# Storing the last sixteen tiles in other pieces: a different spread of short stores over the DMA engines, and another order of the early adds

## The chip, the cores and the metric

The kernel runs on one core of one Trainium2 chip. The metric is the device time of one execution in microseconds (us), as the median of the runs shown. The core has sixteen DMA engines; their queue is fed here by one engine, SyncE (SP), in the order of its program.

## The reference

The kernel computes a batched matrix product with a bias and a residual, all in fp32:

```
x: (16, 512, 1024)   weight: (1024, 768)   bias: (768,)   residual: (16, 512, 768)
out = np.matmul(x, weight) + bias + residual
```

Flattened, that is 8192 rows. It reads 32 MB of x, 24 MB of residual and 3 MB of weights, and it writes 24 MB.

## The kernel before, in words

The 8192 rows are cut into 64 tiles of 128 rows (partitions), and the tiles into four groups S of J = 16. Tile t = 16·S + j. A partition's sixteen rows of a group lie next to each other in memory, so one transfer can load or store any run of tiles j0 to j1 of a group with one contiguous piece per partition. A piece is 4 KB per tile for x and 3 KB per tile for the residual and the output.

Three fixed buffers hold the data. `X` has 16 slots of x. `R` has 32 rows of 768 fp32 values: row t mod 32 holds the residual of tile t, becomes its output in place, and is stored from there. The weights are first loaded into eight rows of `R` from row `W_ROW` on (`w_st`, line 86), and are then cast to bf16 into `w_sb`.

Each tile passes through the same steps. ACT casts x to bf16 (`cast`, L149). PE transposes it as four 128x128 fp32 blocks (`transp`, L157) and VectorE (DVE) copies the result out of PSUM (L158). Sixteen matmuls accumulate into one of three PSUM tiles (`mm`, L164). GpSimd (POOL) adds the bias to the residual row ahead of time (L189), and DVE adds the PSUM result to that row (`finish`, L199).

The first fourteen tiles (`EARLY_END`) are done in another way, because their residuals come late. DVE adds the bias to the PSUM result and puts it in a temporary row of `R` (`tmp(t)`, row 16 + t, L195). POOL later adds that row to the residual row (L185). `ADDS` lists tiles 0 to 15; in it stands the order in which POOL takes those adds. `pool_adds(upto)` is called as the program is written out. It walks that list over the tiles up to `upto`, emits the adds whose inputs have been scheduled, and stops at the first that has not. So the list and the point of the call together decide POOL's order.

All transfers are issued by SP in the order of `ORDER`. The entries are `('x', S, j0, j1)`, `('r', ...)`, `('w', ...)` and `('b', ...)` for loads, and `('s', S, j0, j1)` for a store. A fifth number in a store cuts it into two transfers at that partition. `('c', 3, 15, i)` stores the two column pieces of tile 63, 512 and 256 columns wide (`LAST`). `pump` (L91) emits an entry as soon as what it needs has been emitted. A load into a slot of `R` waits for the add or the store that last used the slot. The load of residual tiles 16 to 21, `('r', 1, 0, 6)`, overwrites the temporary rows of tiles 0 to 5, and so it waits for the adds of these six tiles. The load of tiles 22 to 31 waits for the adds of tiles 6 to 13.

SP works in program order. A transfer that waits holds up every transfer behind it. Transfers that have been issued lie in sixteen queues, one for each DMA engine, and each engine works through its own queue in order.

Of the kernel before, what the change touches and what calls it, by code (L numbers as in the profile page):

```python
# [19 lines left out]
WARM = 12  # L20
EARLY_END = 14
TMP_ROW = 16
W_ROW = 14
ADDS = [10, 14, 3, 2, 4, 15, 11, 1, 5, 13, 7, 6, 12, 9, 0, 8]
HEAD_ORDER = [('cast', 0, 'v'), ('cast', 1, 's'), ('tr', 0), ('tr', 1), ('wc', 0, 0, 's'), ('wc', 0, 1, 'g'),
 ('warm', 3), ('mm', 0, 0), ('mm', 1, 0), ('cast', 2, 'sv'), ('cast', 3, 'sv'), ('warm', 3),
 ('tr', 2), ('tr', 3), ('wc', 1, 0, 's'), ('wc', 1, 1, 'v'), ('mm', 2, 0), ('mm', 0, 1),
# [5 lines left out]
 ('r', 0, 6, 16), ('x', 0, 14, 16), ('x', 1, 0, 6), ('r', 1, 0, 6), ('x', 1, 6, 16),  # L33
 ('r', 1, 6, 16), ('s', 0, 0, 16), ('x', 2, 0, 6), ('r', 2, 0, 6), ('x', 2, 6, 16),
 ('r', 2, 6, 16), ('s', 1, 0, 16), ('x', 3, 0, 6), ('r', 3, 0, 7), ('x', 3, 6, 16),
 ('r', 3, 7, 16), ('s', 2, 0, 16), ('s', 3, 0, 10), ('s', 3, 10, 12, 108), ('s', 3, 12, 14),
 ('s', 3, 14, 15), ('c', 3, 15, 0), ('c', 3, 15, 1)]
LAST = [(0, 512), (512, 256)]


# [1 line left out]
def kernel(  # L42
# [42 lines left out]
    K_ = tc.keep_in_program_order  # L85
    w_st = R[:, W_ROW:W_ROW + 2 * n_q, :]

# [3 lines left out]
    def pump():  # L91
        while queue:
# [7 lines left out]
            elif kind == "r":  # L100
                need = [("store", t - RR) for t in range(J * S + j0, J * S + j1) if t >= RR]
                rows = [t % RR for t in range(J * S + j0, J * S + j1)]
                if S < RR // J and any(W_ROW <= r < W_ROW + 2 * n_q for r in rows):
                    need.append(("wcast", n_q - 1))
# [70 lines left out]

    adds = list(ADDS) + list(range(max(ADDS) + 1, n_t))

# [119 lines left out]
```

## Time and profile before

| | before |
|---|---|
| median of 8 runs | 210.76 us (210.54 to 210.88) |
| the profiled execution | 210.54 us, of which its span is 208.8 us |
| granted TensorE clock, mean | 0.996 |
| PE busy | 202.0 us, 97% of the span |
| POOL, DVE, ACT busy | 115.9, 104.7, 66.1 us |
| the data queue's packets | 87.05 MB, 97.9% of 16 engines' span |
| stores (L130) | ten transfers |

Busy times are the sum of an engine's instructions in one profiled execution. The share of a DMA queue is the time of its packets over the span of all sixteen engines. SPq is SP's queue of DMA issues: a line with it tells when a transfer was ordered, not when its data moved. Span and execution differ by 1.74 us, which lies around the profiled instructions.

### The profile page before, as it was taken

Reading aid. Unit: us, or ns where it says so; the run is one execution under the profiler, and the core shown is the slowest. Engines: PE = TensorE matmul, PEld = TensorE weight load, DVE = VectorE, ACT = ScalarE, POOL = GpSimd, SP = SyncE. Lnnn points to the kernel's source line nnn. Section 1 sums busy time; section 2 is a strip of 40 time slices with the busy share of each in tenths; the row PEclk is TensorE's granted clock in tenths of the full one; section 3 lists DMA queues with packets and bytes.
Section 4 is the critical chain, followed back from the end, with each engine's and each line's share of the span. In section 5 each row is a group of like instructions: output and inputs, shape, how many; then the busy total and the mean of one; then the engine's idle time right before and its main releaser. Section 6 shows DMA issues by size and latency. Waiting matters only on the chain.

```text
span 208.8 us, 3113 instructions
## 1 busy us (share of the span) xinstructions
PE 202.0 (97%) x1298; PEld 130.1 (62%) x1298; DVE 104.7 (50%) x140; ACT 66.1 (32%) x69; POOL 115.9 (56%) x72
## 2 busy tenths in 40 slices
PE   7999999999999999999999999999999999999990
PEld 2455666666666666666666666666666666666660
DVE  0458555445545543654455454645545544654551
ACT  2444513402640372420380094320091046440000
POOL 2100029859999804999029701999207950699400
PEclk9999999999999999999999999999999999999998
DMA  6999999999989899999999999999999999998985
GB/s 234 427 425 433 430 431 453 400 452 420 478 379 488 387 430 413 444 419 427 425 446 457 405 430 471 405 427 405 426 487 411 416 426 468 448 444 371 421 356 203
DMA packets 4780, 87.24 MB, mean 418 GB/s; under 512 B 538, under 2 KB 666, under 8 KB 1694
## 3 DMA queue, kind: packets, MB, share of 16 engines
q1 hardware_dynamic: 4766, 87.05, 97.9%
q8 instruction: 10, 0.16, 0.3%
q14 instruction: 4, 0.03, 0.0%
HBM read 61.88 MB, written 25.17 MB: 417 GB/s over the span
## 4 chain that ended last, share of the span: by engine, by line
PE 92%; DMA 4%; ACT 1%; DVE 1%; SPq 0%; issue 0%
PE psum_o L164 78%; PE pt L157 13%; DMA x_tile<-in_x_dram 4%; PE psum_o L258 1%; ACT xb L146 1%; DVE xt L158 0%; DVE ro L262 0%; SPq L119 0%; SPq L122 0%
## 5 line engine op out<-in xcount | busy, mean ns | idle before, releaser
L164 PE MATMUL psum_o<-w_sb,xt 128*128 128x512 bf16 x1008 | 174.0, 326 | 0.5 <-DVE xt L158 0.3
L164 PEld LDWEIGHTS <-xt 128*128 128x128 bf16 x1008 | 98.5, 98 | 59.2 <-DVE xt L158 0.7
L189 POOL TENSOR_TENSOR ro<-ro,bias_sb 128x768 f32<-128x768 f32 x50 | 88.9, 1823 | 48.4 <-DMA ro<-in_residual_dram 38.0
L149 ACT CAST xb<-x_tile 128x1024 bf16<-128x1024 f32 x60 | 59.7, 1043 | 113.8 <-DMA x_tile<-in_x_dram 87.2
L158 DVE COPY xt<-pt 128x1024 bf16<-128x1024 bf16 x64 | 44.0, 691 | 83.2 <-PE pt L157 83.2
L199 DVE TENSOR_TENSOR ro<-psum_o,ro 128x768 f32<-128x768 f32 x49 | 46.5, 948 | 5.9 <-POOL ro L189 4.8
L185 POOL TENSOR_TENSOR ro<-ro 128x768 f32<-128x768 f32 x14 | 25.0, 1820 | 25.2 <-DMA ro<-in_residual_dram 25.2
L157 PE MATMUL pt<-ident,xb 128*128 128x128 f32 x256 | 38.4, 274 | 0.4 <-ACT xb L146 0.2
L157 PEld LDWEIGHTS pt<-ident,xb 128*128 128x128 f32 x256 | 29.7, 141 | 9.0 <-ACT xb L146 1.1
L195 DVE TENSOR_TENSOR ro<-psum_o,bias_sb 128x768 f32<-128x768 f32 x14 | 13.2, 947 | 0.0
L208 PE MATMUL psum_o<-warm 128*128 128x512 bf16 x12 | 5.0, 602 | 1.2 <-DVE warm_a L204 1.2
L229 ACT CAST w_sb<-ro 128x768 bf16<-128x768 f32 x4 | 3.3, 832 | 3.7 <-DMA ro<-in_weight_dram 3.7
L208 PEld LDWEIGHTS <-warm 128*128 128x128 bf16 x12 | 1.6, 144 | 3.9 <-issue 2.8
L229 POOL CAST w_sb<-ro 128x768 bf16<-128x768 f32 x1 | 0.8, 823 | 5.4 <-DMA ro<-in_weight_dram 5.4
L149 DVE CAST xb<-x_tile 128x1024 bf16<-128x1024 f32 x1 | 0.7, 694 | 4.3 <-DMA x_tile<-in_x_dram 4.3
L146 ACT CAST xb<-x_tile 128x512 bf16<-128x512 f32 x3 | 1.8, 616 | 3.4 <-PE psum_o L164 1.7
L258 PE MATMUL psum_o<-w_sb,xt 128*128 128x512 bf16 (+1 forms) x16 | 2.8, 326 | 0.0
L229 DVE CAST w_sb<-ro 128x768 bf16<-128x768 f32 x3 | 1.7, 557 | 2.0 <-DMA ro<-in_weight_dram 2.0
L147 DVE CAST xb<-x_tile 128x512 bf16<-128x512 f32 x3 | 1.2, 425 | 2.6 <-DMA x_tile<-in_x_dram 2.6
L258 PEld LDWEIGHTS <-xt 128*128 128x128 bf16 x16 | 1.6, 98 | 1.1
L223 PE MATMUL psum_o<-warm 128*128 128x512 bf16 x6 | 1.6, 379 | 0.0
L262 DVE TENSOR_TENSOR ro<-psum_o,ro 128x512 f32<-128x512 f32 (+1 forms) x2 | 1.1, 559 | 0.9 <-PE psum_o L258 0.8
(14 smaller groups left out, 5.1 us busy)
## 6 DMA issues: line engine op xcount, KB each, us to landing
out_dram<-ro SPq DMA_DIRECT2D x3, 6144.0 KB, 34.6
x_tile<-in_x_dram SPq DMA_DIRECT2D x3, 5120.0 KB, 24.1
ro<-in_residual_dram SPq DMA_DIRECT2D x3, 3840.0 KB, 25.6
x_tile<-in_x_dram SPq DMA_DIRECT2D x3, 3072.0 KB, 40.7
ro<-in_residual_dram SPq DMA_DIRECT2D x3, 2304.0 KB, 17.6
x_tile<-in_x_dram SPq DMA_DIRECT2D x4, 1024.0 KB, 8.2
x_tile<-in_x_dram SPq DMA_DIRECT2D x2, 2048.0 KB, 21.2
out_dram<-ro SPq DMA_DIRECT2D x1, 3840.0 KB
```

The lines of the kernel that those rows point to most:

```text
L146: K_(nc.scalar.copy(out=dst[:, 0:K // 2], in_=src[:, 0:K // 2]))
L149: K_((nc.scalar.copy if how == "s" else nc.vector.tensor_copy)(out=dst, in_=src))
L157: K_(nc.tensor.transpose(out=pt[:, q, :], in_=words[:, ts(q, P)], identity=ident))
L158: K_(nc.vector.tensor_copy(out=XT[t % XT_N].rearrange("p q m e -> p (q m e)"), in_=pt.rearrange("p q m -> p (q m)").bitcast(BF16),))
L164: K_(nc.tensor.matmul(PO[t % HEAD][:, n0:n0 + nl], lhsT=XT[t % XT_N][:, q, :, e], rhs=w_sb[:, q, e, n0:n0 + nl], start=(q == 0 and e == 0) ...
L185: K_(nc.gpsimd.tensor_add(out=r, in0=r, in1=tmp(t)))
L189: K_(nc.gpsimd.tensor_add(out=r, in0=r, in1=bias_sb))
L195: K_(nc.vector.tensor_add(out=tmp(t), in0=p, in1=bias_sb))
L199: K_(nc.vector.tensor_add(out=row(t), in0=p, in1=row(t)))
L208: K_(nc.tensor.matmul(PO[0][:, 0:512], lhsT=warm[:, 0:P], rhs=warm, start=True, stop=True))
L229: K_(copy(out=w_sb[:, q, e, :], in_=w_st[:, 2 * q + e, :]))
L258: K_(nc.tensor.matmul(p, lhsT=XT[t % XT_N][:, q, :, e], rhs=w_sb[:, q, e, n0:n0 + nl], start=(q == 0 and e == 0), stop=(q == n_q - 1 and e ...
```

## The change

Three things are edited.

The weights are staged in rows 24 to 31 of `R` rather than in rows 14 to 21.

The list `ADDS` is another permutation of 0 to 15. Written out, POOL's first sixteen adds stood in the order 0, 1, 3, 2, 4, 5, 7, 6, 10, 11, 14, 15, 13, 12, 9, 8. Now they stand in the order 0, 1, 4, 5, 3, 9, 7, 2, 8, 14, 12, 10, 15, 13, 11, 6. From tile 16 on nothing changes.

The stores of the last group (tiles 48 to 63) are cut in other places. Before, tiles 48 to 57 went in one transfer of 128 rows, tiles 58 and 59 as 108 and 20 rows, 60 and 61 in one, 62 in one, and 63 in two column pieces. Now tile 48 goes by itself as 100 and 28 rows, 49 to 52 in one transfer, 53 to 59 in one, 60 and 61 in one, 62 as 126 and 2 rows, and 63 in two column pieces as before. There are twelve stores where there were ten. The instructions of PE, DVE and ACT keep their order.

```diff
-W_ROW = 14
-ADDS = [10, 14, 3, 2, 4, 15, 11, 1, 5, 13, 7, 6, 12, 9, 0, 8]
+W_ROW = 24
+ADDS = [4, 1, 5, 14, 9, 3, 7, 15, 12, 2, 8, 10, 13, 11, 6, 0]
...
- ('r', 3, 7, 16), ('s', 2, 0, 16), ('s', 3, 0, 10), ('s', 3, 10, 12, 108), ('s', 3, 12, 14),
- ('s', 3, 14, 15), ('c', 3, 15, 0), ('c', 3, 15, 1)]
+ ('r', 3, 7, 16), ('s', 2, 0, 16), ('s', 3, 0, 1, 100), ('s', 3, 1, 5), ('s', 3, 5, 12),
+ ('s', 3, 12, 14), ('s', 3, 14, 15, 126), ('c', 3, 15, 0), ('c', 3, 15, 1)]
```

## The prediction

> **What bounds the kernel now.** I read the page's busy shares first, then its slices, then the end of the run in windows, then SP's and POOL's timelines, and last the records of single DMA packets.
>
> ```profile
> PE 202.0 (97%) x1298; PEld 130.1 (62%) x1298; DVE 104.7 (50%) x140; ACT 66.1 (32%) x69; POOL 115.9 (56%) x72
> DMA  6999999999989899999999999999999999998985
> q1 hardware_dynamic: 4766, 87.05, 97.9%
> 204.00:206.00 2.00, 0.02 (x1) 0.00 (x0) 0.42 (x1) 0.00 (x0) 0.00 (x0) 1.00 0.92 363
> 206.00:208.00 2.00, 0.00 (x0) 0.00 (x0) 0.00 (x0) 0.00 (x0) 0.00 (x0) 0.78 0.20 73
> SPq L292 <- DMA out_dram<-ro: 2.8, 1, 2.8
> ```
>
> Two resources are full: PE, and the sixteen DMA engines. PE's last matmul ends at 204.03 us. A window's columns are its length, the busy time of PE, weight loads, DVE, ACT and POOL, the granted clock, DMA share and GB/s: the DMA engines are still 92% busy after PE's end. SP's last wait of 2.8 us is for stores. So the end is set by the DMA engine that finishes last.
>
> Which one that is can be worked out. A packet record has start, duration and size, but no engine. On a busy engine each packet starts 3 or 4 ns before the recorded end of the one before it, so the 4,766 packets fall into sixteen chains. From 13 us until 199 us no chain is idle, except for ten gaps of about 1.05 us and four of 0.3 us. Each of the ten is one 16,384-byte instruction packet on queue 8 (at 23.1, 40.5, 59.8, 79.9, 98.3, 118.8, 137.6, 158.0, 176.4 and 196.0 us). They hit eight chains in turn; the ninth falls on the chain of the first, the tenth on that of the second.
>
> Short stores tell where a chain stands. The 108 rows land in twelve steps and the 20 rows in ten: the number of engines is the largest divisor of the rows up to 16. The ten lie among the twelve. I number the places 0 to 15 so that short transfers fill the lowest. The chains that end last (data end, us):
>
> - A, among places 0 to 9: 207.24, and B, there too: 207.21.
> - The rest of places 0 to 9: 205.8 to 206.7. Places 10 and 11: 206.41 and 206.28.
> - Places 12 to 15: D 206.37 (hit by fetches 1 and 9), E 205.95 (2 and 10), F 205.89 (8), G 205.85 (none; idle for 2.64 us at 199 us).
>
> From A's end to the span's end (208.75) it takes 1.51 us: landing, SP's remaining waits, the closing.
>
> **The stores.** One tile-row (3 KB) takes 0.118 us as a packet of its own (the 3,072-byte stores take 121 ns, overlapping by 3), 0.115 us in a pair (234 ns) and 0.1135 us in ten (1,138 ns). I count tile-rows against eight per engine and tile. Before, tiles 58 and 59 give places 0–9 +6, 10–11 +2, 12–15 −16. Now 100 rows should fall on ten engines, 28 on fourteen, 126 on fourteen, 2 on two. Tile 48 then gives places 0–9 +4, 10–13 −6, 14–15 −8, and tile 62 gives 0–1 +2, 2–13 +1, 14–15 −8. Net change: places 0–1 get 0, 2–9 −1, 10–11 −7, 12–13 **+11**, 14–15 0.
>
> A and B end 0.12 us earlier, or not at all if at place 0 or 1: 207.1 to 207.24. The relief goes mainly to places that did not end last. What counts is who stands at 12 and 13. Fetches 6 and 7 hit places 10 and 11, fetch 8 hits F, 9 hits D, 10 hits E, and 3 to 5 hit places below 10. Eight engines in turn, read as neighbours, are 7 to 14: F is 12, D 13, E 14, G 15. G fits: at the store of tiles 60–61 the idle F gets its first packet 0.035 us before the idle G. So D gets the +11.
>
> D's chain, which has no idle time to absorb it: the third big store ends at 193.46. Then, with 6 ns for each completion: tile 48, 2 × 0.118 + 0.006 = 0.24; tiles 49–52, eight packets of 12 KB at 0.456 (interpolated between 0.2305 and 1.134) = 3.66; tiles 53–59, eight at 0.795 (the 21,504-byte loads took 0.799) = 6.37; tiles 60–61, 1.85; tile 62, 9 × 0.118 = 1.07; the pieces of tile 63, 0.65 and 0.345, as now. Sum 193.46 + 14.19 = 207.65. That is 0.41 past A's 207.24; with the rounding 0.40. F gets as much more, but its 1.5 us of idle time at the end absorb it.
>
> SP's orders at the end (start, duration), and the shortest, median and longest order of a store in ns:
>
> ```profile
> 188.29 0.34 SPq L130 DMA_DIRECT2D out_dram<-ro  x1
> 194.37 1.62 SPq L130 DMA_DIRECT2D out_dram<-ro  x2
> 200.44 2.43 SPq L130 DMA_DIRECT2D out_dram<-ro  x2
> L130 SPq DMA_DIRECT2D out_dram<-ro x10: 332/344/1222, 62.3 to 204.5; - x10
> ```
>
> The Trainium skill speaks against the worry about D. "Runtime: NRT & Kernel Launch", section "Instruction fetch mechanics", says that PE's instructions are refilled in 16 KiB blocks and that crossing a block is mostly hidden. For PE the trace agrees; for the DMA engine that carries the block it shows 1.05 us each time. By the rule alone D would be 2.1 us earlier and the sum would be A's: no change.
>
> **Issues.** SP orders two transfers more. The 28 rows go out at about 161 us and SP is next needed at 173: nothing. The 2 rows stand ahead of the first piece of tile 63 (203.97 us) on SP. A second half costs between the median issue, 0.34 us, and that of the 20 rows, 1.22 us; I take the latter as the nearest row. From 202.9 us it holds SP to 204.15, so the piece goes out 0.2 us later, the last one 0.1. D reaches that piece at 206.65 only, so it is hidden; uncovered it would cost 0.1 to 0.2.
>
> Tiles 53–57 now wait for tile 59 (ordered at 194.37 rather than 188.29). The earliest chain runs out at 189.66 + 1.42 + 3.66 = 194.7 and first packets come 0.83 to 1.28 us after an order. The fastest chains idle 0.5 to 0.9 us; they end at 205.8 to 206.4 now and stay ahead. D gets there at 197.4.
>
> **The adds.** They decide when SP may order residual tiles 16–21.
>
> ```profile
> 40.75 0.33 SPq L124 DMA_DIRECT2D ro<-in_residual_dram  x1
> 48.53 0.33 SPq L122 DMA_DIRECT2D x_tile<-in_x_dram  x1
> 61.86 0.33 SPq L124 DMA_DIRECT2D ro<-in_residual_dram  x1
> 44.06 7.12 POOL L185 TENSOR_TENSOR ro<-ro 128x768 f32<-128x768 f32 x4 [3.34 <-DMA ro<-in_residual_dram]
> 61.77 10.69 POOL L189 TENSOR_TENSOR ro<-ro,bias_sb 128x768 f32<-128x768 f32 x6
> ```
>
> Tile 2's add now stands behind those of 9 and 7, which wait for the residuals landing at 43.9. It ends at 44.06 + 3 × 1.78 = 49.4, so that load goes out at 49.4 rather than 40.75. Behind it on SP wait x tiles 22–31 (48.53, now 49.85), then the next residuals, the first big store and more x. The DMA engines have x tiles 16–21 queued until 51.3 (first chain) to 53.3 (D); packets arrive at 50.3 to 50.7. Cover 0.6 us; D's is 2.6. So nothing; without the cover, its shortfall.
>
> The `61.77` line is the first bias add of the next tiles. The last early add, tile 6, ends at 44.06 + 11 × 1.78 = 63.6 (61.77 before). The next residual load and the store go out 1.8 us later; x tiles 22–31 keep the engines busy until 69: nothing. Tile 16's add ends at 65.4 instead of 63.6, and DVE's finish of tile 16 waits for it until 66.35. Behind that on DVE stands tile 19's PSUM copy (67.05), which PE needs at 68.15: 1.1 us of slack.
>
> **The staging rows.** The load of residuals 6–15 no longer waits for two weight casts. It went out at 11.79, when its semaphore's earlier transfer, a weight load, had landed at 11.69; the casts of 7.4 to 8.2 us were over. Zero.
>
> **Sum:** +0.40 on the profiled 210.54 gives 210.94. That execution lies 0.22 below the median; on the median 210.76 it is 211.16. A measurement of this kernel can tell about 0.2% (0.42 us) from no change, so this lies right at the edge.
>
> **The rivals.** (1) D stands at place 14 or 15. Against it: the order of the fetches. Then A or B sets the end, at 207.1 to 207.24, and the time is 210.6 to 210.75, no slower; it decides as soon as D is not at 12 or 13. (2) The middle runs dry: POOL or an order is over 0.6 us later than reckoned, the DMA engines idle, and PE waits. D's cushion speaks against it; the price is some 0.5 to 1 us more, 211.6 to 212.2. (3) The pieces do not confine themselves to ten or fourteen engines but use all sixteen. Then A loses 6 tile-rows and D gains 16 × 0.117 = 1.87, ending at 208.24: +1.0, 211.76. The landings of the 108 rows (twelve) and the 20 rows (ten) speak against it. The Trainium skill ("DMA: Bandwidth & Descriptors", section "Rules for kernel authors") has such a rule: two transfers of disjoint halves of the partitions both use all sixteen engines and are not worth it; by it the sum would be this rival's. (4) The slow loads repeat differently: D lost 0.56 us in the load at 69 to 80 us, B 0.9 us after 189 us. Then ±0.3.
>
> **How the numbers follow.** Forecast 0.62, rival 1 0.16, rival 2 0.10, rival 3 0.06, rival 4 0.06. The forecast's own range is 210.85 to 211.5 (±0.3 from rival 4's sizes); it splits evenly at +0.42: 0.31 slower, 0.31 same. Rival 1 gives same 0.12, faster 0.03, slower 0.01. Rivals 2 and 3 are slower, 0.16. Rival 4 gives faster 0.04, same 0.02. Sum: faster 0.07, same 0.45, slower 0.48. The range takes in rivals 1 and 3: 210.6 to 211.8.
>
> **What would show it.** In the trace after: landings of ten, fourteen, fourteen and two; the chain hit by fetches 1 and 9 ending last, near 207.65, with nine packets of tile 62; SP's order of residuals 16–21 at 49.4 and no idle chain at 51; PE's end at 204.0. The prediction is wrong if that chain carries no packet of tile 62, if the last landing comes under 207.3 or over 208.5 us, or if PE ends later.

## The result, and the profile after

The changed kernel is slower: 211.89 us as the median of 11 runs (211.53 to 212.15), beside 210.75 us for the kernel before on the same chip (31 runs, 210.46 to 211.73). The ratio is 1.0052, 95% interval 1.0043 to 1.0061. The forecast was 211.16 us with a range of 210.6 to 211.8; the time lies just above that range and 0.73 us above the number. The profiled execution took 211.68 us, of which its span is 209.87.

The page of the kernel after, busy shares, DMA slices and the data queue:

```profile
PE 201.6 (96%) x1298; PEld 129.9 (62%) x1298; DVE 104.7 (50%) x140; ACT 66.1 (32%) x69; POOL 115.9 (55%) x72
DMA  6999999999999999999999999999999999998994
q1 hardware_dynamic: 4912, 87.05, 97.7%
```

The same two resources are full and the bytes are the same. There are 146 packets more. The end of the run in windows (length, PE, weight loads, DVE, ACT, POOL, granted clock, DMA share, GB/s), kernel after:

```profile
204.00:206.00 2.00, 0.56 (x6) 0.26 (x3) 0.91 (x2) 0.00 (x0) 0.00 (x0) 1.00 0.88 296
206.00:208.00 2.00, 0.00 (x0) 0.00 (x0) 0.00 (x0) 0.00 (x0) 0.00 (x0) 1.00 0.55 203
208.00:210.00 2.00, 0.00 (x0) 0.00 (x0) 0.00 (x0) 0.00 (x0) 0.00 (x0) 0.81 0.02 8
```

Two things differ from before. PE still works until 204.56 us (before, 204.02). And the DMA engines are 88% busy in the first window but move 296 GB/s, where before they were 92% busy and moved 363: the packets that fill this stretch are long for their size. In the next window the share is 0.55 instead of 0.20. SP's last wait is again for stores:

```profile
SPq L292 <- DMA out_dram<-ro: 3.4, 2, 3.1
```

SP's orders and POOL's adds in the first 70 us, kernel after (start, duration, what, and the idle time before it with its cause):

```profile
49.38 0.33 SPq L124 DMA_DIRECT2D ro<-in_residual_dram  x1
49.87 0.33 SPq L122 DMA_DIRECT2D x_tile<-in_x_dram  x1
63.56 0.33 SPq L124 DMA_DIRECT2D ro<-in_residual_dram  x1
```
```profile
43.99 7.13 POOL L185 TENSOR_TENSOR ro<-ro 128x768 f32<-128x768 f32 x4 [5.09 <-DMA ro<-in_residual_dram]
...
58.18 5.36 POOL L185 TENSOR_TENSOR ro<-ro 128x768 f32<-128x768 f32 x3
63.48 10.68 POOL L189 TENSOR_TENSOR ro<-ro,bias_sb 128x768 f32<-128x768 f32 x6
```

These moved as reckoned: residual tiles 16 to 21 go out at 49.38 (49.4 was forecast), the x tiles behind them at 49.87 (49.85), POOL's first bias add of the next tiles starts at 63.48 (63.6).

The packet chains answer for the rest. I rebuilt them as in the prediction, in this kernel and in most of the others; where two packets start within a nanosecond a chain can be swapped with another, so I use them for the chains that stand out. The chain of fetches 1 and 9, D, carries two rows of tile 48 and nine packets of tile 62, and so is at places 10 to 13, as inferred. Its third big store ends at 193.97 us, its data at 208.14. But it does not end last. A chain at places 0 to 9 ends at 208.53. It holds two packets of tiles 60 and 61 (6,144 bytes, 234 ns as a rule) that took 441 and 1,114 ns, at 204.85 and 205.33 us, while tile 62's pieces were being written.

### The profile page after: what moved, and what is told of

Read it like the earlier page. It is cut to its first block, busy times and chain, and to the rows that moved or that the text cites. A ratio compares the mean times of both kernels' runs of the same rounds, so it can differ in the third digit from the quotient of the medians.

```text
span 209.9 us, 3116 instructions
## 1 busy us (share of the span) xinstructions
PE 201.6 (96%) x1298; PEld 129.9 (62%) x1298; DVE 104.7 (50%) x140; ACT 66.1 (32%) x69; POOL 115.9 (55%) x72
## 4 chain that ended last, share of the span: by engine, by line
PE 92%; DMA 4%; DVE 1%; SPq 0%; ACT 0%; issue 0%
PE psum_o L164 78%; PE pt L157 13%; DMA x_tile<-in_x_dram 4%; PE psum_o L258 1%; DVE xt L158 0%; ACT xb L146 0%; DVE ro L262 0%; SPq L119 0%; SPq L122 0%
## 5 line engine op out<-in xcount | busy, mean ns | idle before, releaser
L208 PE MATMUL psum_o<-warm 128*128 128x512 bf16 x12 | 4.4, 538 | 1.2 <-DVE warm_a L204 1.2
L223 PE MATMUL psum_o<-warm 128*128 128x512 bf16 x6 | 1.6, 379 | 0.0
```

What stands on the lines that cost most here:

```text
L208: K_(nc.tensor.matmul(PO[0][:, 0:512], lhsT=warm[:, 0:P], rhs=warm, start=True, stop=True))
```

## The experiments

Two theories stood first. **Just in time:** tile 2's add, moved behind those of 9 and 7, lets SP order residual tiles 16 to 21 only when they are needed; that costs in spite of the cover that the prediction counted. **The stores:** the account of tile-rows holds, and the rest comes from the pieces of the last tiles. Each kernel is told by its edit to the kernel before or after. Ratios are to the kernel before on the same chip, with a 95% interval; a count of executions over 211.2 us goes with them. Of the kernel before's own executions in these comparisons 12 of 162 lie above that.

### Parts alone, and one part taken out: e1_stores, e2_adds, e3_rows, e4_62whole, e_after2

e1_stores is before with the `ORDER` of after. e2_adds is before with the `ADDS` of after. e3_rows is before with `W_ROW = 24`. e_after2 is the kernel after again. e4_62whole is after with

```diff
-('s', 3, 14, 15, 126)
+('s', 3, 14, 15)
```

> The stores are cut as in the changed kernel; the order of the adds and the staging rows are those of before. Theory 'spread' (the cut loads the DMA engine at place 13, hit by fetches 1 and 9, with 11 tile-rows more): that engine ends at 207.65 us instead of 206.37 and the time rises by 0.4 to 0.5 us over the kernel before. Theory 'small pieces' (the fourteen-engine store of tile 62 makes packets around it slow: in the changed kernel one packet of tiles 60 and 61 took 1,114 ns instead of 234 on the chain that ended last): the whole 1.1 us comes with the stores, +0.9 to +1.3 us, and packets of 3,072 bytes between 204 and 206 us again take 200 to 400 ns instead of 121. Theory 'middle' (the order of the adds lengthens the stall of the loads at 77 to 79 us, which took 0.5 us more from that engine): the stores bring at most the 0.4 us, and the third big store ends on that engine at 193.5 as before, not at 194.0.

> Only POOL's order of the first sixteen adds is that of the changed kernel; stores and staging rows are those of before. Theory 'middle': the load of residual tiles 22 to 31 is ordered at 63.6 us and stalls as in the changed kernel (9.8 us of excess over the sixteen engines instead of 3.2), the slowest landing comes at 81.4 instead of 80.9 us, and the time rises by 0.2 to 0.5 us. Theories 'spread' and 'small pieces': the adds are hidden, the time stays within 0.1 us of before. If the stall at 77 to 79 us is of no kernel's making, its size here is anything between the two and the time within 0.2 us.

> The changed kernel with tile 62 stored whole (128 rows on sixteen engines); all else as changed. Theory 'small pieces': no packet after 204 us takes over 200 ns more than its like, the last-ending chain is that at place 13, at about 208.0, and the time falls by 0.4 to 0.6 us against the changed kernel (211.3 to 211.5). Theory 'spread' alone: place 13 carries 8 tile-rows of tile 62 instead of 9, so 0.12 us less; 211.7 to 211.8. Theory 'middle': as 'spread'.

> The changed kernel again, for a second profile on the chip of the other runs. If the stall of the loads at 77 to 79 us (9.8 us of excess over sixteen engines) and the slow packet of 1,114 ns at 205.3 us belong to the kernel, both come again, and the time is 1.0 to 1.3 us above before. If they belong to one execution, this profile has a smaller stall or none after 204 us, place 13 ends last near 207.7 to 208.1, and the median stays about 1.1 us above before all the same only if other executions have their own.

> The kernel before with the weights staged in rows 24 to 31 (W_ROW = 24) and nothing else. Stores alone cost 0.09%, the adds' order alone 0.25%, and the whole change 0.5 to 0.6%: some 0.2% are left. Theory that the rows do nothing: 1.000, within 0.001; the first loads go out at the same times and the 0.2% come from the parts together. Rival, the rows carry the rest (the load of residual tiles 6 to 15 goes out at another time and shifts the first loads): 1.002, and PE's start or the landings at the head are seen later.

| kernel | median us | ratio | interval | over 211.2 |
|---|---|---|---|---|
| e1_stores | 210.82 | 1.0009 | 0.9996 to 1.0022 | 4 of 12 |
| e2_adds | 211.24 | 1.0025 | 1.0014 to 1.0035 | 7 of 11 |
| e3_rows | 210.64 | 0.9994 | 0.9984 to 1.0004 | 0 of 11 |
| e4_62whole | 210.95 | 1.0019 | 1.0005 to 1.0032 | 2 of 12 |
| e_after2 | 211.82 | 1.0059 | 1.0043 to 1.0075 | 4 of 4 |

The staging rows cost nothing. The order of the adds, which the prediction put at nothing, costs 0.25% by itself, about 0.53 us. The stores alone show hardly more than their noise, and less than either price expected of them (0.4 us from D, 0.9 us and more from small pieces). And taking only tile 62's cut out of the whole change brings the ratio from 1.0052 or 1.0059 to 1.0019.

One thing that the adds change is seen at tile 32. The timeline of the kernel before, ACT's casts of x and PE's transposes:

```profile
102.75 2.94 ACT L149 CAST xb<-x_tile 128x1024 bf16<-128x1024 f32 x3 [12.20 <-DMA x_tile<-in_x_dram]
...
103.99 0.60 PE L157 MATMUL pt<-ident,xb 128*128 128x128 f32 x4
```

The same in e2_adds:

```profile
103.39 1.99 ACT L149 CAST xb<-x_tile 128x1024 bf16<-128x1024 f32 x2 [12.82 <-DMA x_tile<-in_x_dram]
...
104.49 0.66 PE L157 MATMUL pt<-ident,xb 128*128 128x128 f32 x4 [0.31 <-ACT xb L149]
```

ACT waits 12 us for x tiles 32 to 37 in both. In e2_adds they come 0.64 us later, and PE's transposes wait 0.31 us for the cast, where before they waited for nothing. PE's last matmul ends at 204.68 us instead of 204.02. A cast takes 0.98 us, so before it ended at about 103.73, and PE's weight loads for that tile began at 103.89: PE had some 0.16 us of slack there.

This wait is not by itself the cost. e10_adds_early (next section) takes as long as the kernel before, and PE's weight loads wait there too:

```profile
103.06 2.94 ACT L149 CAST xb<-x_tile 128x1024 bf16<-128x1024 f32 x3 [12.66 <-DMA x_tile<-in_x_dram]
...
104.16 0.42 PEld L157 LDWEIGHTS pt<-ident,xb 128*128 128x128 f32 x4 [0.54 <-ACT xb L149]
```

PE ends at 204.35 us there. And in the profiles of e_after2 and e5_48whole, both long executions with the late order, the cast starts at 102.74 and 102.72 as before and PE waits for nothing at tile 32. Where the wait is long, it shows in the time. In the profiled execution of e9_64and64, the longest of that kernel (212.64 us), the cast starts at 105.06, PE waits 1.99 us for it and ends at 206.34, and most of the sixteen chains of DMA packets stand idle for 0.9 to 2.4 us from about 195 us on.

### When the residuals are ordered: e10_adds_early, e11_adds_mid

Both are the kernel before with another list, and in both residuals 22 to 31 go out later than before. In e10_adds_early tile 2's add is sixth, in e11_adds_mid tile 5's is seventh.

```diff
-ADDS = [10, 14, 3, 2, 4, 15, 11, 1, 5, 13, 7, 6, 12, 9, 0, 8]
+ADDS = [4, 1, 5, 3, 2, 14, 9, 7, 15, 12, 8, 10, 13, 11, 6, 0]   # e10_adds_early
+ADDS = [10, 14, 3, 2, 4, 15, 11, 1, 7, 5, 13, 6, 12, 9, 0, 8]   # e11_adds_mid
```

> The kernel before with the changed order of the adds, but tile 2's add moved ahead of those of 9 and 7 (0, 1, 4, 5, 3, 2, 9, 7, 8, 14, 12, 10, 15, 13, 11, 6). SP can order residual tiles 16 to 21 at 40.75 us again and tiles 22 to 31 at about 61.9 us. The order with tile 2 late gave +0.25%, a stall of the loads at 77 to 79 us of 10 us in excess over sixteen engines, and a PE wait of 0.47 us at tile 32. Theory 'late order' (it is the late order of the residual loads that costs): the stall falls to 1 to 3 us in excess, PE does not wait at tile 32, the time is within 0.1% of before. Theory 'the permutation itself' (which rows POOL touches when): the time stays 0.2 to 0.3% above before.

> The kernel before with POOL's order 0, 1, 3, 2, 4, 7, 5, 6, 10, 11, 14, 15, 13, 12, 9, 8: tile 5's add stands behind that of tile 7. SP orders residual tiles 16 to 21 at 47.6 us, 3.7 us before the DMA engines run out of x tiles 16 to 21 (51.3), and tiles 22 to 31, the first big store and x tiles 32 to 37 at 63.6 us and after, 1.8 us later than before. Theory 'just in time' (the cost comes from ordering residual tiles 16 to 21 at 49.4, when the engines are about to run out): the time is that of before, no slow packets at 52 us and 1 to 3 us of stall at 77 to 79. Theory 'late second half' (the cost comes from ordering tiles 22 to 31 and what follows 1.8 us later): the stall is 4 to 16 us in excess and the time 0.2 to 0.3% above before.

SP's orders in e10_adds_early:

```profile
40.44 0.33 SPq L124 DMA_DIRECT2D ro<-in_residual_dram  x1
48.34 0.33 SPq L122 DMA_DIRECT2D x_tile<-in_x_dram  x1
```

and in e11_adds_mid:

```profile
47.44 0.33 SPq L124 DMA_DIRECT2D ro<-in_residual_dram  x1
48.28 0.33 SPq L122 DMA_DIRECT2D x_tile<-in_x_dram  x1
63.40 0.33 SPq L124 DMA_DIRECT2D ro<-in_residual_dram  x1
```

e10_adds_early: 210.57 us, 0.9996 (0.9988 to 1.0005). e11_adds_mid: 210.69 us, 0.9999 (0.9990 to 1.0007). Neither has an execution over 211.2. So an order at 47.44 us costs nothing and one at 49.38, with the x tiles moved to 49.87, costs 0.25%; which of these two later orders costs was not separated. Ordering residuals 22 to 31 at 63.4 rather than 61.9 is free, as was forecast, and so is POOL's later end: DVE's finishes wait for POOL as long in e11_adds_mid as in after, and e11_adds_mid loses nothing by it. One expectation failed in both: the packets of residuals 22 to 31 lost 8 and 9 us beyond their usual time at 74 to 80.5 us, summed over the engines, where 1 to 3 were expected, and in e10_adds_early PE was not to wait at tile 32. The waits, of after and then of e11_adds_mid (us in all, times, longest):

```profile
DVE ro L199 <- POOL ro L189: 6.7, 6, 2.2
```
```profile
DVE ro L199 <- POOL ro L189: 7.0, 6, 2.4
```

### The cut of tile 62: e9_64and64, e6_62only, e5_48whole, e12_after_early

e9_64and64 is after with tile 62 cut at 64 instead of 126. e6_62only is before with tile 62 cut at 126. e5_48whole is after with tile 48 whole. e12_after_early is after with e10_adds_early's list.

```diff
-('s', 3, 14, 15, 126)
+('s', 3, 14, 15, 64)      # e9_64and64, to after
-('s', 3, 14, 15)
+('s', 3, 14, 15, 126)     # e6_62only, to before
-('s', 3, 0, 1, 100)
+('s', 3, 0, 1)            # e5_48whole, to after
```

> The changed kernel with tile 62 cut at row 64 instead of 126: two pieces of 64 rows, each on all sixteen engines with 4 rows, as many transfers and packets of the same size as before the cut was moved. Tile 62 stored whole gave 210.95 us beside 211.82 for the changed kernel. Theory 'uneven spread' (packets become slow when engines carry rows other than those the even spread gives them, 9 rows on fourteen engines): the slow packets after 204 us are gone and the time is that of the whole store, 210.9 to 211.2 us. Theory 'two pieces' (two transfers in flight instead of one make the packets slow): the slow packets stay and the time is 211.5 to 211.9 us.

> The kernel before with tile 62 stored as 126 and 2 rows and nothing else. By the account of tile-rows the places 0 and 1 get two tile-rows more, 2 to 13 one more, 14 and 15 eight fewer: +0.12 us, ratio 1.0006. Theory that the uneven pieces themselves are slow (packets of 3 and 6 KB taking longer at 204 to 206 us, one 6 KB packet nearly 0.9 us more): 1.002 to 1.004, with such a packet on a chain of a low place in the trace. Rival, the split costs only together with tile 48's early pieces: 1.0006 or less and no long packet.

> The kernel after with tile 48 stored by all 128 rows at once. By the account of tile-rows, against after the places 0 to 9 lose four, 10 to 13 gain six, 14 and 15 gain eight: the chain at place 13 ends 6 x 0.117 = 0.7 us later, at about 208.4 to 208.8, the chains at low places 0.47 us earlier: ratio 1.005 to 1.007. If it is the pieces of tile 62 meeting late data that set the end on a low place, and place 13 stays under it: 1.003.

> The kernel after with tile 2's add moved back among the first five (order 0, 1, 4, 5, 3, 2, 9, 7, 8, 14, 12, 10, 15, 13, 11, 6), so that residual tiles 16 to 21 are ordered at about 40.5 us. If the cost of the adds is the order given just in time, and the rows do nothing, this is the kernel with the stores alone: 1.001. If the stores cost more together with the rows, or with the other order of adds: 1.003. If the order at 49.4 us were not the cause: 1.005, as after.

| kernel | median us | ratio | interval | over 211.2 |
|---|---|---|---|---|
| e9_64and64 | 211.31 | 1.0027 | 1.0012 to 1.0041 | 7 of 12 |
| e6_62only | 210.91 | 1.0018 | 1.0000 to 1.0036 | 5 of 12 |
| e5_48whole | 211.65 | 1.0042 | 1.0027 to 1.0057 | 5 of 5 |
| e12_after_early | 211.47 | 1.0028 | 1.0009 to 1.0047 | 8 of 12 |

Two transfers of 64 rows recover as much as no cut at all would, within the intervals, though 211.31 us lies above the 210.9 to 211.2 that was expected: the second transfer is not what costs. e5_48whole was a test of the account. Its chain D takes eight rows of tile 48 instead of two, 0.95 us instead of 0.24. Its third big store ends at 193.38, and 193.38 + 14.19 + 0.71 = 208.28; its data ends at 208.26, and there D is the last chain. The ratio came out under the 1.005 to 1.007 that I expected. In the profiled execution D started that sum earlier than the 193.97 of after; whether it did in the others is not known.

e12_after_early was a surprise. I expected e1_stores again, 1.001. Its executions fall into two sorts: four from 210.55 to 210.73, eight from 211.24 to 212.19. The profiled one was the shortest of all, 210.55, and shows nothing amiss on the chain that ended last. So two more executions were profiled, and the cut was varied.

### Even and uneven cuts: e13_early_62whole, e14_early_64and64, e15_early_104, and profiles of the long executions

All are e12_after_early with another cut of tile 62. e12b_look and e12c_look are e12_after_early itself, e15b_look is e15_early_104 itself.

```diff
-('s', 3, 14, 15, 126)
+('s', 3, 14, 15)          # e13_early_62whole
+('s', 3, 14, 15, 64)      # e14_early_64and64
+('s', 3, 14, 15, 104)     # e15_early_104
```

> The kernel of e12_after_early (rows 24 to 31, early adds with tile 2's among the first five, tile 48 in two pieces, 49 to 52, 53 to 59) with tile 62 stored whole. e12_after_early spread from 210.55 to 212.19 us, and its profiled execution (210.55) showed the account's end and nothing more. Theory that the uneven pieces of tile 62 make the long executions: these go away, all runs lie between 210.4 and 211.1; the account against the kernel before is low places -2 tile-rows (-0.23 us), place 13 +10, its chain ending at about 193.3 + 14.19 - 0.12 = 207.4: ratio 1.0000 to 1.001. Rival, the pieces of tile 48 or the two middle transfers make them: half of the runs stay above 211.2, ratio 1.002 to 1.003.

> The same with tile 62 as 64 and 64 rows: two transfers as in the kernel after, but both spread evenly, four rows on each of sixteen engines. Theory of the uneven spread: as with tile 62 whole, 1.000 to 1.001, and no run above 211.2. Rival, the second order itself (0.3 to 0.5 us on SP ahead of tile 63's first piece) or any second transfer costs it: 1.002 to 1.003 and half of the runs long.

> e12_after_early once more, to look into one of its long executions (8 of 12 were over 211.2 us). If it is long: by the theory of tile 62's pieces PE ends by 204.1 us, place 13 ends where its third big store's end + 14.17 puts it, and a chain of a low place ends later than that with a packet of 3 to 6 KB of tiles 60 to 62 some 0.5 to 1.5 us too long. By the rival (loads repeat slower) the third big store's end on place 13's chain lies over 193.9 us.

> As e12b_look: a second chance of a long execution, with the same two readings.

> The kernel of e12_after_early with tile 62 cut at 104 rather than at 126: 104 rows on thirteen engines, eight each, and 24 on twelve, two each. With tile 62 whole (e13_early_62whole) or as 64 and 64 the ratio was 1.000 and no packet of 6 KB after 203 us took over 0.27 us; cut at 126 it was 1.003 and such packets took 0.39 to 1.12 us in five profiles. By the account against e13_early_62whole, places 0 to 11 get two tile-rows more (+0.23 us), place 13 eight fewer: ratio 1.000 to 1.001. Theory that any uneven spread makes long packets: at least one packet of 6 KB takes over 0.35 us after 203 us, some runs lie above 211.2, ratio 1.002 to 1.004. Rival, it is the cut at 126 or the two-row piece: no such packet, 1.000 to 1.001.

> e15_early_104 once more, to look into one of its long executions (7 of 12 were over 211.4 us; its profiled one, 210.69, had no packet of 6 KB over 0.27 us after 203 us). Theory of the uneven spread: if this execution is over 211.2 us, the chain that ends last holds one or more packets of 3 to 6 KB that take 0.5 to 1 us too long between 203.5 and 206.5 us; if it is under 210.9 us, none. Rival: a long execution without such a packet, PE's end or the third big store's end being late instead.

Ratios by the order of the adds and by tile 62's pieces; rows 24 to 31, tile 48's pieces and the middle are as in after in all of them:

| | whole | 64 and 64 | 126 and 2 | 104 and 24 |
|---|---|---|---|---|
| tile 2's add early (order at 40.6 us) | 0.9995 (0.9986 to 1.0004) | 0.9999 (0.9990 to 1.0008) | 1.0028 | 1.0029 (1.0010 to 1.0048) |
| as in after (49.4 us) | 1.0019 | 1.0027 | 1.0052, 1.0059 | not run |

In the upper row no execution of the even spreads is over 211.2 us (0 of 22), and 15 of 24 of the uneven ones are. The upper row ran on three chips, but the chip alone is not the reason: e12b_look and e12c_look ran beside the even spreads on theirs, and both were long (212.12 and 211.25 us, where the even spreads took 210.37 to 210.96). The two causes add: 0.0024 for the late order with tile 62 whole, 0.0033 for the cut with the early order, together 0.0057. The size of the cut's part is not settled: with the add order of before it was only 0.0009 in e1_stores and 0.0018 in e6_62only.

The chain that ended last, by execution (us; ns for packets):

```
kernel              time    its third big   packets over 0.4 us that should take    data
                            store ends      0.12 (3 KB) or 0.23 (6 KB)              end
e12_after_early     210.55  193.15 (D)      none                                    207.32
e13_early_62whole   210.59  193.30 (D)      none                                    207.36
e14_early_64and64   210.53  191.52          none                                    207.24
e15_early_104       210.69  191.45          none                                    207.40
e12c_look           211.25  191.55          6 KB 1,109 at 204.91                    208.08
after               211.68  192.02          6 KB 441 at 204.85, 1,114 at 205.33     208.53
e_after2            211.81  191.20          3 KB 562 at 191.55, 6 KB 476 at 204.91  208.62
                                            and 1,120 at 205.42
e12b_look           212.12  192.61          6 KB 661 at 205.50, 684 at 206.16       208.92
e15b_look           212.35  192.84          6 KB 1,011 at 205.95                    209.17
```

The three further profiles all met a long execution, and each has such a packet on its last chain, while tile 62's pieces are being written. D ends where the account puts it: in e12b_look 193.40 + 14.17 = 207.57, and its data ends at 207.57. In the two longest the third big store on the last chain ended about 1 us later as well: it holds a packet of 2.2 us, where 1.8 is usual. Every profile has such a packet in that store, right behind an 8,192-byte instruction packet of 0.31 us on another queue; in these two it lies on the chain that ends last. That is a second term, and the rival's, though on a low place and not on D. In the ten profiles with tile 62 whole or as 64 and 64, no 6 KB packet that started more than 1 us after tile 62's first order took over 0.28 us. Five of the six profiled 126-and-2 executions that were over 211 us had one of 0.66 to 1.12 us (e5_48whole, where D was last, had 0.42). A short one, e6_62only at 210.75 us, had one of 0.60. Earlier, at 199 to 203 us, the kernel before has long 6 KB packets too (up to 0.77 us), while its own uneven pieces, the 108 and 20 rows of tiles 58 and 59, are written; the chains that end last hold none of them.

The windows show the loss. e13_early_62whole:

```profile
204.00:206.00 2.00, 0.09 (x1) 0.00 (x0) 0.43 (x2) 0.00 (x0) 0.00 (x0) 1.00 0.92 364
206.00:208.00 2.00, 0.00 (x0) 0.00 (x0) 0.00 (x0) 0.00 (x0) 0.00 (x0) 0.63 0.21 77
```

e12b_look, the same program but for tile 62's cut, PE ending at 204.02 in it:

```profile
204.00:206.00 2.00, 0.03 (x1) 0.00 (x0) 0.42 (x1) 0.00 (x0) 0.00 (x0) 1.00 0.77 272
206.00:208.00 2.00, 0.00 (x0) 0.00 (x0) 0.00 (x0) 0.00 (x0) 0.00 (x0) 0.75 0.51 176
```

364 GB/s against 272 in the same 2 us: about 0.18 MB that is left for later, and PE has no part in it. Not all of it is long packets. The share falls from 0.92 to 0.77: some engines stand idle in e12b_look, since tile 63's first piece, whose order took 1.13 us on SP, sends its first packet at 205.64 instead of 204.87. At full share the rate would be 396 and 353 GB/s. The chain that ended last was not among the idle ones.

Two more expectations failed here. e15_early_104's first profile, one of the short executions, had no long packet, though its times already spread like e12_after_early's; only e15b_look showed one. And e1_stores, which has the same cut, was over 211.2 us in 4 of 12 executions where e12_after_early was in 8 of 12; whether that is chance, I can't tell.

### One cut that pays: v1_104

The kernel before with tiles 58 and 59 cut at 104 instead of 108:

```diff
-('s', 3, 10, 12, 108)
+('s', 3, 10, 12, 104)
```

> The kernel before with tiles 58 and 59 cut at row 104 instead of 108: 104 rows on thirteen engines (8 each), 24 rows on twelve (2 each). Against the even spread places 0 to 11 get +4 tile-rows, place 12 none, 13 to 15 -16; before it was +6 for 0 to 9, +2 for 10 and 11, -16 for 12 to 15. The two chains that end last stand at places 0 to 9 and lose 2 tile-rows: 207.24 becomes 207.0, the engine at place 12 gets +16 and ends near 206.2. Theory 'spread': 0.1 to 0.2 us faster than before. Theory 'uneven spread' (slow packets): the same, since 104 rows are spread unevenly as 108 were; at most 0.2 us either way.

210.48 us (210.24 to 210.88), ratio 0.9989, interval 0.9981 to 0.9998: it is shorter than both kernels, by little. By the account a low place gets 8 + 2 = 10 tile-rows of each of the two tiles instead of 9 + 2 = 11. Two tile-rows less are 0.23 us, and 0.0011 × 210.7 is 0.23; the interval allows 0.04 to 0.40 us, so that they agree so closely is partly luck.

## Why the prediction was wrong

"Slower" had the largest chance, 0.48 beside 0.45 for the same, but the size was short by 0.73 us, and the time fell out of the range. In the profiled execution: D's sum began 0.51 us later than reckoned (193.97 for 193.46), was right to 0.02 (14.17 for 14.19), a low chain then ended 0.39 past D, and 0.17 less passed from the last data to the end of the span (1.34 us for 1.51). Together +0.71, and 211.68 - 210.94 is 0.74.

**Where D stands, and the account of tile-rows: right.** D is at 10 to 13, E (fetches 2 and 10) at 14 or 15, tile 62 falls on fourteen engines and two, and D's tail took 14.17 us. Rival 3, all sixteen engines, is refuted by the packets: nine packets of 126 rows on each of fourteen chains, none of them on the other two. The rule that the prediction set beside it, of the Trainium skill ("DMA: Bandwidth & Descriptors", section "Rules for kernel authors"), speaks of halves and does not carry over to cuts like these. For halves, 64 and 64 rows, the runs agree that nothing is gained (0.9999 against 0.9995 whole). Rival 1 is refuted by D's place. In e5_48whole D's end came out by the account to 0.02 us.

**"Cover 0.6 us; D's is 2.6. So nothing": the first step that failed.** The order of residuals 16 to 21 moved as forecast, and I asked only whether an engine would run dry at 51 us. It cost 0.24 to 0.28% all the same, with four kinds of stores (e2_adds against before, and after, e4_62whole and e9_64and64 against their kernels with the early order). By which path is open. In after no engine was idle at 51 us; in e9_64and64 0.7 us was lost there, summed over the sixteen. What followed was later data: the load of residuals 22 to 31, where packets are slow at 77 to 80 us, lost 4.5 to 16 us between 74 and 80.5 us, summed over the engines, in the six profiles with the late order. Without it ten profiles lost 0.2 to 3.2, e15b_look 6.0. But on one chip, that of e10_adds_early, e11_adds_mid and v1_104, 7 to 9 us were lost without the late order, and these three kernels are not slower for it; with it e9_64and64 lost 14 there. D came out of its third big store at 193.4 to 194.0 us, and once at 195.25 (in e4_62whole, whose profiled execution also started late, PE's first matmul of the product at 9.20 us instead of 8.23), against 192.9 to 193.6 without. The two overlap. Why the late order makes those packets slower, and how much of its cost comes through them, is not shown.

**The slack of x at tile 32: a step that was missing.** I took PE's feed for safe ("PE's end at 204.0"; PE's later end was listed as what would prove it wrong). Its slack at that tile was some 0.16 us. In after it waited there:

```profile
103.27 2.94 ACT L149 CAST xb<-x_tile 128x1024 bf16<-128x1024 f32 x3 [12.44 <-DMA x_tile<-in_x_dram]
...
104.36 0.42 PEld L157 LDWEIGHTS pt<-ident,xb 128*128 128x128 f32 x4 [0.32 <-ACT xb L149]
```

PE's weight loads for the tile started at 104.36 instead of 103.89 us, and PE ended at 204.56. (The head was 0.3 us later in this execution, PE's first matmul of the product at 8.53 against 8.23; that shortened the wait.) How much of the time comes from PE's later end is not shown: in e10_adds_early PE waited there and ended at 204.35, at 0.9996. Rival 2 (PE waits, 211.6 to 212.2) thus held the right time for a part of the right reason: PE waited, but because x came late, and no engine had run dry at 51 us in this execution.

**"A and B end 0.12 us earlier, or not at all": the second step that failed.** The sum had tile-rows at 0.118 us each whatever else was being written. With tile 62 on fourteen engines and two, packets of 6 KB that overlap it took up to 1.12 us, and a low chain ended at 208.53, not at 207.1 to 207.24. That step is worth 0.33% (e12_after_early against e13_early_62whole) to 0.40% (e_after2 against e4_62whole), but only 0.09 to 0.18% in e1_stores and e6_62only. A price on the spread of a store, beside its tile-rows, was in no rival.

**The second half's order: mis-sized.** I took 1.22 us, the nearest row; it took 0.29. Kernel after, shortest, median and longest order of a store (ns):

```profile
L130 SPq DMA_DIRECT2D out_dram<-ro x12: 294/344/366, 64.0 to 205.1; - x12
```

It was hidden either way, since D had no gap before tile 63's pieces. **The staging rows, the last add and the middle transfers** cost nothing, as forecast (e3_rows 0.9994, e13_early_62whole 0.9995); the fast chains idled 0.2 to 1.9 us until about 195.8 where I had 0.5 to 0.9, and did not end last.

**The +0.40 from D: mis-sized.** With the two failed steps removed, in e13_early_62whole, the rest of the change neither costs nor gains (0.9995, at most 1.0004). By the account its D ends at 193.31 + 14.19 - 0.12 = 207.38, and D is the chain that ended last there, at 207.36. That is only 0.12 past the 207.24 of A. D's start of that sum moves by up to 0.7 us from one execution to the next even without the late order (192.94 to 193.64), so the forecast's +0.40, worked out from a single profile, was no larger than that spread.

## What to carry to other kernels

An account of bytes per DMA engine placed a chain to 0.02 us, but only as far as packets keep their time: count what a store does to its neighbours by trying an even and an uneven cut of the same transfer. A load moved to the point where it is "just needed" should be tried alone, at an early and at a late order: neither a queue that stays busy nor a single wait of the engine that reads the data told its cost here. When a kernel's times spread, profile several executions before naming a cause: the first profile of e12_after_early showed nothing.

## What was not expected of the hardware

- Pieces of a store that fall on fourteen engines and two, or on thirteen and twelve, made single packets of 6 KB last 0.66 to 1.12 us instead of 0.23, in some executions and not in others; evenly spread pieces, 64 and 64, slowed many 3 KB packets by 0.1 us and more in both profiles (the longest took 0.45 and 0.52 us instead of 0.12) and lengthened no 6 KB packet past 0.27 us. What makes the difference inside the chip is open.
- SP's order of a store takes 0.34 us as a rule. The 20-row second half took 1.22 us in the kernel before, and in two long executions, e12b_look and e15b_look, other orders took over 1 us:

```profile
L130 SPq DMA_DIRECT2D out_dram<-ro x12: 294/344/1131, 62.8 to 205.2; - x12
```
```profile
L130 SPq DMA_DIRECT2D out_dram<-ro x12: 325/349/1492, 62.7 to 205.9; - x12
```

In e12b_look it is the order of tile 63's first piece at 203.98; in e15b_look it is the second piece of tile 62 at 203.15, and tile 63's first piece took 1.06 us too. The longest order of after, 0.37 us, shows that a long execution does not need one. Whether the long order and the long packets have one cause was not tried.
